# Sums of squares as float32r pairs: how the RMS statistics of a two-layer trunk are summed over partitions

## The chip, the cores and the metric

The kernel runs on one core of one Trainium2 chip. The metric is the device time of one execution in microseconds (us); of several executions the median is given. Before the change it is 2197.2 us (three runs, 2195.38 to 2199.59). PE is TensorE's matrix unit, PEld its weight loads, DVE is VectorE, ACT ScalarE, POOL GpSimd, SP the engine that issues most transfers.

## The reference

A trunk of two layers over 1024 tokens of width 1024, in float32. Layer 0 mixes tokens by latent attention (a projection to 512 + 256 + 64 columns, RMS norms of the first two parts, rotary keys, eight heads); layer 1 by an mLSTM matrix memory with four heads. Each is followed by a gated MLP with a causal convolution of width 3. Every part begins with an RMS norm and a shift and scale from the condition c, and a final norm ends the trunk:

```python
def rms_norm(x, gain=None):
    x32 = x.astype(jnp.float32)
    y = x32 * lax.rsqrt(jnp.mean(x32 * x32, axis=-1, keepdims=True) + EPS)

for i in range(DEPTH):
    h = rms_norm(x) * (1 + sc_a) + sh_a
    y = mla_mixer(h, ...) if i % N_MIXERS == 0 else mlstm_mixer(h, ...)
    x = x + g_a * y
    h = rms_norm(x) * (1 + sc_f) + sh_f
    x = x + g_f * conv_ffn(h, ...)
return rms_norm(x, final_norm)
```

The change concerns how the mean of squares in `rms_norm` is computed.

## The kernel before, in words

Activations lie transposed: 128 of the 1024 features on the partitions, tokens along the columns, eight tiles to a row block. The tokens are worked on in two halves of 512 (`hf` 0 and 1), the final norm of the second half in two groups of 256 columns. Float32 products are made of three float32r products in `mm3` (L175 to L177): each operand is split into a float32r part (`hi`) and the rest (`lo`), and hi by hi, hi by lo and lo by hi are summed in PSUM. The MLP multiplies in a form of Strassen's scheme with operands named `T1` to `T4`, `B11` and so on; its partial results carry the names `da`, `db`, `pa`, `pd`.

For a norm the sum over features runs over partitions and tiles. A `Squares` object holds a running sum `ssq` of 128 x 512: ScalarE squares a tile, VectorE adds it. The last square of a half may be kept apart (`keep`) and not added. Then `rstd_cols` forms, for each block of 128 tokens, products of `ssq` (as the weight) with a column of ones, and of the kept squares with the same column, into the PSUM tile `st` (L250): tokens now lie on partitions. VectorE makes the variance of it (`var`, L254), POOL raises it to -1/2 (`rstd`, L255), and `to_rows` transposes it, spread over 128 rows, into the tile `rb` (L262), by which VectorE multiplies the activations. These places, in order of time: `x_rows`, the norm of the input, once for each half (45 and 78 us); the norms of the query and key-value parts in `in_norms` (75 to 110 us: L494 adds a bias, L495 and L496 write the normed `cqn` and `ckvn`); both halves of the out-projection of each layer; both halves of the end of each MLP.

What sets the order: `later(n, fn, key)` queues work, here sums or transposes, and `mm3` counts the queue down by one per call, so that `fn` is emitted n sets of three products later. The counts are constants: `AFTER_SSQ`, `XW` (input norm of the second half: sums, transposes), `W0` and `WF` (MLP ends of layers 0 and 1, for each half), `X_WAIT` (out-projections), and `EVAC` (input projection: the accumulators' emptying). A tile scheduler then orders the instructions of each engine by dependences and its own priorities, so emitted order is not final order. In the part from 75 to 101 us all tiles `st` and `rb` come from a pool with one PSUM bank. The seven accumulators `ia` of the input projection are emptied by VectorE (L444, each times the row `rbs`), and the rotary query product `qrp` behind them takes a bank that one of them held. The weights for these products are split when they arrive: `whi` by ScalarE (L167) and `wlo` by VectorE (L168). At the end, L1671 multiplies the result by `rb` and the output goes out.

Of the kernel before, what the change touches and what calls it, by code (L numbers as in the profile page):

```python
# [29 lines left out]
KSCALE = 128 ** -0.5  # L30
NEG = -3.0e38
AFTER_SSQ = 6
EVAC = (7, 9)
INNER = 5
EARLY = 2

# [2 lines left out]
SCALE_ACT = ((0, 0), (1, 0), (1, 1))  # L39

STEPS = "nspppnspppoooonmooso", "nnsposppooponpmspoopo"
XW = (4, 2)
WARM = 14
W0, W0_RSTD, WF, WF_RSTD = (6, 10), (4, 3), (4, 5), (4, 4)
SHARE = 7
GATES = (2, 18, 22, 26)
MODS = (0,) * 4 + (2,) * 11 + (3,)
# [4 lines left out]
K_SHIFT = 0  # L52
AFTER_RSTD = 3
AHEAD, LOOK, RAWS, MRAWS = 4, (7, 5), 5, 2
X_WAIT, X_RSTD = (12, 3), (8, 3)
TURN = 2


# [39 lines left out]
def trunk_kernel(ctx: ExitStack, tc: tile.TileContext, xT, pos, c_d, cols_d, mod_w, win, winT, w0, w1, wf, wd, out):  # L98
# [39 lines left out]
    make_identity(nc, ident)  # L138
    ones = cst.tile([P, 1], F32, name="ones")
    pool.memset(ones, 1.0)  # L140
    nhalf = cst.tile([P, 4], F32, name="nhalf")
    pool.memset(nhalf, -0.5)
    modc = [cst.tile([P, 48], F32, name=f"modc{i}") for i in range(2)]
# [72 lines left out]
    class Squares:  # L216


        def __init__(self, p, w=HS, share=False, bufs=2, eng=None, pin=False, sqs=2):
            tile_ = lambda tag, n, size=HS: p.tile([P, size], F32, tag=f"{tag}{size}", bufs=n, name=nm(tag))[:, 0:w]  # L220
            self.w, self.n, self.share, self.eng, self.pin = w, 0, share, eng or dve, pin
            self.t = tile_("ssq", bufs, w)
            self.sq = lambda: tile_("sq", sqs, w)
            self.more = []

        def keep(self, x):

# [4 lines left out]
        def add(self, x, **kw):  # L232
# [4 lines left out]
            else:  # L237
# [2 lines left out]
                eng = pool if self.share and self.n % 2 and self.n < SHARE else self.eng  # L240
                pin(eng.tensor_tensor(self.t, self.t, sq, ALU.add))

    def rstd_cols(ssq, n, ps=None):

        st = (ps or mm_tile)("st")
        nt = ssq.w // P
        for t in range(nt):
            terms = [ssq.t, *ssq.more]
            for i, v in enumerate(terms):
                pe.matmul(st[:, t:t + 1], v[:, t * P:(t + 1) * P], ones, start=i == 0, stop=i == len(terms) - 1)  # L250
        var = cst.tile([P, 4], F32, tag="var", bufs=2, name=nm("var"))
        rstd = cst.tile([P, 4], F32, tag="rstd", bufs=2, name=nm("rstd"))
        with tc.high_priority():
            dve.tensor_scalar(var[:, 0:nt], st[:, 0:nt], 1.0 / n, EPS, ALU.mult, ALU.add)  # L254
            pool.tensor_tensor(rstd[:, 0:nt], var[:, 0:nt], nhalf[:, 0:nt], ALU.pow)  # L255
        return rstd
# [8 lines left out]
    def rstd_later(ssq, n, key, then, wait=None, ps=None, turn=AFTER_RSTD):  # L265

        def cols_():
            rstd = rstd_cols(ssq, n, ps)
            later(turn, lambda: then(to_rows(rstd, ssq.w, ps)), key)
        later(wait or AFTER_SSQ, cols_, key)  # L270

    def norm_k(p, x, rb, l, j, k, hhi, hlo):
# [228 lines left out]
    def in_norms(hf, raw, ev, ps):  # L501

        sq = [Squares(ev, bufs=4), Squares(ev, bufs=4)]
        for m in range(6):
            sq[m // 4].add(raw[:, m, :], bias=inb[:, m:m + 1])
        def rope_key():
            sl = slice(hf * HS, (hf + 1) * HS)
            t = raw[:, 6, :]
            act.activation(t, t, AF.Identity, bias=inb[:, 6:7])
            rope_apply(t, raw[:, 7, :], hf)  # L510
            act.activation(kkh[:, sl], t, AF.Copy)
            dve.tensor_tensor(kkl[:, sl], t, kkh[:, sl].bitcast(F32), ALU.subtract)
# [64 lines left out]
    class Ev:  # L577
# [292 lines left out]
    def out_proj(px, psC, osrc, us, w, l, early=0):  # L870
# [7 lines left out]
        for hf in range(2):  # L878
# [3 lines left out]
            for m in range(KT):  # L882
# [82 lines left out]
    def mlp(px, psC, T, l, u_d, pd, done, cols, extra=None, scaled=None):  # L965
# [222 lines left out]
        def d_run(i, p, w, t0=0, width=HS):  # L1188
# [14 lines left out]
            if g == len(DG) - 1 and op in ("B22", "T3", "B21", "T4"):  # L1203
                for c0, cw_ in ((0, HS),) if hf == 0 else cols:
                    if t0 <= c0 < t0 + width:
                        if (hf, c0) not in stats:
                            stats[hf, c0] = Squares(pd[0], cw_, bufs=sum(c[1] == cw_ for c in ((0, HS), *cols)),
                                                    sqs=2 if cw_ == HS else 4)
                        with tc.high_priority():
# [572 lines left out]
```

## Time and profile before

| | before |
|---|---|
| median of three runs | 2197.2 us |
| profiled execution, span | 2200.1 us (2.9 us above the median) |
| PE busy | 2166.5 us, 98% |
| DVE busy | 1693.1 us, 77% |
| ACT busy | 1046.7 us, 48% |
| POOL busy | 178.3 us, 8% |
| products into `st` for the statistics | 180 pairs of load and matmul |

The profile shows one execution of its own; its span stands for that execution's time. A row of a group gives line, engine, operation, the tile that is written and the tiles read, then a count, durations and forms. A row of a timeline gives a start, the length of the stretch to the end of the last instruction in it, and, in square brackets, the idle time of the engine ahead of it with what ended the wait. Matmul durations overlap, so the cost of one is read from start to start.

### The profile page before, as it was taken

The page shows a single profiled execution, that of the slowest core. Times are in us where ns is not written, and L with a number is a line of the kernel's source. Part 1 is how long each engine was busy: PE and PEld are TensorE (multiplying, and loading weights), DVE is VectorE, ACT ScalarE, POOL GpSimd, SP SyncE. Part 2 cuts the span into 40 slices and gives each one's busy share as a digit, 9 for nine tenths or more (in the row PEclk, how much of TensorE's full clock was granted, in tenths as well). Part 3 has the DMA queues.
Part 4 walks back from the last instruction along what each step waited for, and adds up shares of the span by engine and source line. Part 5 has one row for each costly group of instructions (what it writes and reads, how often), then busy time and mean ns, then how long its engine had stood idle before and what let it go on. Part 6 is the DMA issues. An engine that isn't in the chain of part 4 may idle for free.

```text
span 2200.1 us, 28740 instructions
## 1 busy us (share of the span) xinstructions
PE 2166.5 (98%) x10557; PEld 1818.0 (83%) x10557; DVE 1693.1 (77%) x2769; ACT 1046.7 (48%) x1812; POOL 178.3 (8%) x216
## 2 busy tenths in 40 slices
PE   9999999999999999999999999999999999999998
PEld 7878888787888888877888888988788888887787
DVE  8877878669878777899973655566887777778997
ACT  6465556446544444543453434344554444453335
POOL 0000000000000000042210111010000000002232
PEclk9999999999999999999999999999999999999999
DMA  8512234832444332542132243444143332245122
GB/s 317 152 50 63 92 109 142 285 125 69 157 139 143 123 125 85 204 151 89 53 121 93 62 131 103 132 157 171 64 144 101 111 120 92 79 163 194 50 80 77
DMA packets 105085, 270.50 MB, mean 123 GB/s; under 512 B 12336, under 2 KB 15984, under 8 KB 104944
## 3 DMA queue, kind: packets, MB, share of 16 engines
q1 hardware_dynamic: 104544, 268.28, 36.9%
q8 instruction: 83, 1.36, 0.3%
q14 instruction: 58, 0.48, 0.1%
q10 hardware_dynamic: 400, 0.39, 0.1%
HBM read 221.53 MB, written 44.47 MB: 121 GB/s over the span
## 4 chain that ended last, share of the span: by engine, by line
PE 85%; DVE 9%; DMA 3%; ACT 2%; issue 1%; POOL 0%; SPq 0%; POOLq 0%; DVEq 0%; ACTq 0%
PE pa L175 7%; PE pa L177 7%; PE pa L176 7%; PE pd L177 3%; PE pd L175 3%; PE pd L176 3%; PE sc L673 3%; PE op L175 3%; PE op L176 3%; PE op L177 2%; PE inp L177 2%; PE da L175 2%; PE inp L175 2%; PE inp L176 2%; PE da L176 2%; PE db L175 2%
## 5 line engine op out<-in xcount | busy, mean ns | idle before, releaser
L988 ACT ACTIVATE whi<-raw 128x512 fp32r<-128x512 f32 (+1 forms) x252 | 147.3, 607 | 243.2 <-PE pb L176 61.0
L988 ACT ACTIVATE whi<-wsum 128x512 fp32r<-128x512 f32 (+1 forms) x224 | 134.0, 617 | 181.8 <-PE pa L176 61.5
L175 PE MATMUL pa<-T,whi 128*128 128x512 f32 x528 | 205.9, 390 | 0.0
L176 PE MATMUL pa<-T,whi 128*128 128x512 f32 x528 | 205.4, 389 | 0.0
L177 PE MATMUL pa<-T,wlo 128*128 128x512 f32 x528 | 205.1, 389 | 0.0
L989 DVE TENSOR_TENSOR wlo<-wsum,whi 128x512 fp32r<-128x512 f32 (+1 forms) x224 | 151.1, 690 | 32.8 <-ACT whi L988 31.5
L989 POOL TENSOR_TENSOR wlo<-raw,whi 128x512 fp32r<-128x512 f32 (+1 forms) x80 | 119.9, 1515 | 401.7 <-ACT whi L988 394.0
L175 PE MATMUL da<-U,whi 128*128 128x512 f32 (+1 forms) x364 | 139.5, 383 | 3.4 <-DVE x L294 3.4
L177 PE MATMUL da<-U,wlo 128*128 128x512 f32 (+1 forms) x364 | 138.4, 383 | 2.0 <-DVE wlo L989 2.0
L176 PE MATMUL da<-U,whi 128*128 128x512 f32 (+1 forms) x364 | 139.2, 382 | 0.0
L989 DVE TENSOR_TENSOR wlo<-raw,whi 128x512 fp32r<-128x512 f32 (+1 forms) x172 | 115.7, 679 | 24.9 <-ACT whi L988 24.9
L167 ACT ACTIVATE whi<-wraw 128x1024 fp32r<-128x1024 f32 x67 | 70.7, 1059 | 117.1 <-PE op L176 59.2
L175 PEld LDWEIGHTS pa<-T,whi 128*128 128x128 f32 x528 | 99.1, 188 | 22.2 <-ACT whi L988 1.2
L177 PEld LDWEIGHTS pa<-T,wlo 128*128 128x128 f32 x528 | 99.1, 188 | 20.6
L176 PEld LDWEIGHTS pa<-T,whi 128*128 128x128 f32 x528 | 99.1, 188 | 20.3
L1140 DVE TENSOR_TENSOR U<-q,U 128x1024 fp32r<-128x1024 f32 x84 | 102.9, 1241 | 14.0 <-ACT U L1139 13.6
L1028 ACT ACTIVATE ct<-a,cols 128x512 f32<-128x512 f32 x88 | 70.8, 808 | 83.9 <-DVE a L1050 47.9
L175 PE MATMUL db<-U,whi 128*128 128x512 f32 x264 | 103.3, 391 | 1.3 <-ACT whi L988 1.3
L168 DVE TENSOR_TENSOR wlo<-wraw,whi 128x1024 fp32r<-128x1024 f32 x67 | 81.7, 1222 | 29.4 <-ACT whi L167 27.2
L177 PE MATMUL db<-U,wlo 128*128 128x512 f32 x264 | 102.9, 390 | 0.0
L176 PE MATMUL db<-U,whi 128*128 128x512 f32 x264 | 102.8, 389 | 0.0
L1139 ACT ACTIVATE U<-q 128x1024 fp32r<-128x1024 f32 x84 | 79.7, 979 | 47.7 <-DVE q L1138 22.2
(378 smaller groups left out, 6097.3 us busy)
## 6 DMA issues: line engine op xcount, KB each, us to landing
raw<-in_wf SPq DMA_DIRECT2D x96, 512.0 KB, 4.0
wraw<-in_w SPq DMA_DIRECT2D x67, 512.0 KB, 3.7
mraw<-in_mod_w SPq DMA_DIRECT2D x56, 512.0 KB, 4.0
ud<-ct SPq DMA_DIRECT2D x88, 256.0 KB, 2.4
q<-ud SPq DMA_DIRECT2D x88, 256.0 KB, 4.6
raw<-in_wd SPq DMA_DIRECT2D x32, 512.0 KB, 6.4
pa<-in_mod_w SPq DMA_DIRECT2D x24, 512.0 KB, 3.7
x<-xd SPq DMA_DIRECT2D x48, 256.0 KB, 4.8
```

The costliest lines, as they stand in the source:

```text
L167: act.activation(hi, raw, AF.Copy)
L168: dve.tensor_tensor(lo, raw, hi.bitcast(F32), ALU.subtract)
L175: pe.matmul(ps, lh, rh, start=first, stop=False, skip_group_check=more)
L176: pe.matmul(ps[:, 0:rl.shape[-1]], lh, rl, start=False, stop=False, skip_group_check=more)
L177: pe.matmul(ps, ll, rh, start=False, stop=last, skip_group_check=more)
L673: pe.matmul(ps[:, cs], a[:, qs if n < 3 else qrs_], b[:, cs], start=n == 0, stop=n == 4)
L988: act.activation(hi, src, AF.Copy)
L989: eng.tensor_tensor(lo, src, hi.bitcast(F32), ALU.subtract)
L1028: act.activation(t, a[:, 2:], AF.Identity, bias=col(f"cb{l}", m), scale=cw(m, 2))
L1139: act.activation(hi, w, AF.Copy)
L1140: dve.tensor_tensor(lo, w, hi.bitcast(F32), ALU.subtract)
```

## The change

The running sum is split into a float32r part and its rest, both in one tile `shl` (ScalarE copies, VectorE subtracts), and its sum over partitions is made by two float32r products per block with `ones2`, two columns of ones, in place of one f32 product with one column. A kept square still has its f32 product, with one column. The columns of `st` lie two apart. The last square of first halves (out-projection and MLP end of both layers) is no longer kept but added by VectorE; that of second halves stays kept, and the two last groups of 256 columns stay f32 throughout. Five constants of the order are raised, and a pool is opened earlier, so that the tile `shl` of the second half's norms can be in it.

```diff
-EVAC = (7, 9)
+EVAC = (9, 11)
-XW = (4, 2)
+XW = (6, 4)
-W0, W0_RSTD, WF, WF_RSTD = (6, 10), (4, 3), (4, 5), (4, 4)
+W0, W0_RSTD, WF, WF_RSTD = (9, 10), (4, 3), (7, 5), (4, 4)
-X_WAIT, X_RSTD = (12, 3), (8, 3)
+X_WAIT, X_RSTD = (15, 3), (8, 3)
...
+    ones2 = cst.tile([P, 2], F32R, name="ones2")
+    act.activation(ones2, ones.to_broadcast([P, 2]), AF.Copy)
...
+        def split(self):
+
+            room, tag, bufs = self.room
+            t = room.tile([P, 1024], F32R, tag=tag, bufs=bufs, name=nm("shl"))
+            hi, lo = [t[:, i * HS:i * HS + self.w] for i in range(2)]
+            act.activation(hi, self.t, AF.Copy)
+            dve.tensor_tensor(lo, self.t, hi.bitcast(F32), ALU.subtract)
+            self.pair = hi, lo
...
+        terms = [(v, ones2) for v in ssq.pair] if ssq.pair else [(ssq.t, ones)]
+        terms += [(v, ones) for v in ssq.more]
         for t in range(nt):
-            terms = [ssq.t, *ssq.more]
-            for i, v in enumerate(terms):
-                pe.matmul(st[:, t:t + 1], v[:, t * P:(t + 1) * P], ones, start=i == 0, stop=i == len(terms) - 1)
+            for i, (v, one_) in enumerate(terms):
+                pe.matmul(st[:, 2 * t:2 * t + one_.shape[-1]], v[:, t * P:(t + 1) * P], one_, start=i == 0,
+                          stop=i == len(terms) - 1, skip_group_check=len(terms) > 2)
...
+        if not ssq.more:
+            ssq.split()
         later(wait or AFTER_SSQ, cols_, key)
...
+        if hf == 1:
+            sq[0].room = sq[1].room = pa, "shl", 1
...
+    stA, pa = phase("pa", side="right")
     in_norms(1, rawB, Ev(), None)
-    stA, pa = phase("pa", side="right")
...
-                ssq.keep(x[:, m, :]) if m == KT - 1 else ssq.add(x[:, m, :])
+                if hf and m == KT - 1:
+                    ssq.split()
+                    ssq.keep(x[:, m, :])
+                else:
+                    ssq.add(x[:, m, :])
...
-                            if op in ("T3", "T4") and (p == 3 or p == 2 and c0 > 0):
+                            if op == "T4" and (p == 3 or p == 2 and c0 > 0):
+                                if cw_ == HS:
+                                    stats[hf, c0].split()
                                 stats[hf, c0].keep(xs[hf][:, m, c0:c0 + cw_])
```

The rows below are the order of one engine's instructions in the built program. A row has the line, the operation, the tile written and the tiles read (with a number for each tile) and the size; lines of the changed kernel are some 2 to 23 higher.

TensorE in the input projection of the second half, at the sums of squares of the query part (`st_690`, then `st_716`) and the key-value part (`st_707`, `st_735`) and of the second half's input norm (`st_716`, then `st_748`), to the first transposes. Before:

```order
L250 MATMUL st_690<-ones,ssq_641 128x1 x4
L177 MATMUL ia_502<-h_458,winl_107 128x512
L175 MATMUL ia_503<-h_458,winh_106 128x512
L176 MATMUL ia_503<-h_459,winh_106 128x512
L250 MATMUL st_707<-ones,ssq_642 128x1 x4
L177 MATMUL ia_503<-h_458,winl_107 128x512
L175 MATMUL ia_504<-h_458,winh_106 128x512
L250 MATMUL st_716<-ones,ssq_115 128x1 x4
L176 MATMUL ia_504<-h_459,winh_106 128x512
L177 MATMUL ia_504<-h_458,winl_107 128x512
L262 MATMUL rb_728<-ident,rstd_696 128x128 x4
```

and after, with the rows between left out from the second sums on:

```order
L262 MATMUL st_716<-ones_77,shl_678 128x2
L178 MATMUL ia_513<-h_461,winh_108 128x512
L179 MATMUL ia_513<-h_460,winl_109 128x512
L177 MATMUL ia_514<-h_460,winh_108 128x512
L262 MATMUL st_716<-ones_77,shl_678 128x2 x7
...
L262 MATMUL st_735<-ones_77,shl_681 128x2 x7
...
L262 MATMUL st_748<-ones_77,shl_707 128x2 x7
L177 MATMUL ia_512<-h_460,winh_110 128x512
L178 MATMUL ia_512<-h_461,winh_110 128x512
L276 MATMUL rb_764<-ident,rstd_726 128x128 x4
```

Each sum is now eight products instead of four, the first of them ahead of the other seven, with wide products between; counted over the projection, the first `rb` stands 17 wide products later. The second half's input norm has its `rb` between the last wide products before, and behind all of them, directly ahead of the first `qrp`, after.

VectorE from the first use of `rb` to the emptying of the accumulators. Before:

```order
L494 SCALAR_TENSOR_TENSOR raw_470<-raw_470,inb,rb_751 128x512
L168 TENSOR_TENSOR wlo_784<-wraw_781,whi_783 128x1024
L168 TENSOR_TENSOR wlo_790<-wraw_787,whi_789 128x1024
L496 SCALAR_TENSOR_TENSOR ckvn_668<-raw_470,cols,ckvn_668 128x512
L494 SCALAR_TENSOR_TENSOR raw_470<-raw_470,inb,rb_751 128x512
L496 SCALAR_TENSOR_TENSOR ckvn_668<-raw_470,cols,ckvn_668 128x512
L444 TENSOR_TENSOR raw_843<-ia_500,rbs_767 128x512
```

and after:

```order
L170 TENSOR_TENSOR wlo_826<-wraw_823,whi_825 128x1024
L512 SCALAR_TENSOR_TENSOR ckvn_677<-raw_479,cols,ckvn_677 128x512
L494 TENSOR_TENSOR raw_479<-raw_479,cs_638 128x512
L495 TENSOR_TENSOR raw_479<-raw_479,cs_639 128x512
L510 SCALAR_TENSOR_TENSOR raw_479<-raw_479,inb,rb_787 128x512
L496 TENSOR_TENSOR raw_479<-raw_479 128x512
L170 TENSOR_TENSOR wlo_1589<-wraw_1586,whi_1588 128x1024
L512 SCALAR_TENSOR_TENSOR ckvn_677<-raw_479,cols,ckvn_677 128x512
L460 TENSOR_TENSOR raw_873<-ia_509,rbs_803 128x512
```

L444 became L460. Ahead of the first of them now stand four weight rests (`wlo`, two of them above the rows shown) instead of two, and the three rotary steps of the key (L494 to L496 of the changed kernel, which stood behind the emptying as L478 to L480).

VectorE at the end of the program, where `rb_18782` and `rb_18863` belong to the first group of 256 columns, `rb_18821` and `rb_18902` to the second. Before:

```order
L1671 TENSOR_TENSOR x_17142<-x_17142,rb_18637 128x1024
L294 SCALAR_TENSOR_TENSOR x_17070<-da_18289,modc_80,x_17070 128x256
L1671 TENSOR_TENSOR x_17070<-x_17070,rb_18782 128x2x256 x2
L254 TENSOR_SCALAR var_18817<-st_18810 128x2
L1671 TENSOR_TENSOR x_17070<-x_17070,rb_18782 128x2x256 x2
L1671 TENSOR_TENSOR x_17070<-x_17070,rb_18821 128x2x256 x4
```

and after:

```order
L268 TENSOR_SCALAR var_18842<-st_18837 128x2
L243 TENSOR_TENSOR ssq_18670<-ssq_18670,sq_18850 128x256
L1694 TENSOR_TENSOR x_17219<-x_17219,rb_18737 128x1024
L268 TENSOR_SCALAR var_18898<-st_18891 128x2
L1694 TENSOR_TENSOR x_17147<-x_17147,rb_18863 128x2x256 x4
L1694 TENSOR_TENSOR x_17147<-x_17147,rb_18902 128x2x256 x4
```

The first group's four products, of which two stood ahead of the second group's variance, now all stand behind it.

More of the change, by code (lines that the diff above doesn't have):

```diff
@@ L223, in __init__ @@
             self.sq = lambda: tile_("sq", sqs, w)
-            self.more = []
+            self.more, self.pair, self.room = [], None, (p, "shl", 1)
         def keep(self, x):
@@ L246, in rstd_cols @@
         nt = ssq.w // P
+        terms = [(v, ones2) for v in ssq.pair] if ssq.pair else [(ssq.t, ones)]
+        terms += [(v, ones) for v in ssq.more]
         for t in range(nt):
-            terms = [ssq.t, *ssq.more]
-            for i, v in enumerate(terms):
-                pe.matmul(st[:, t:t + 1], v[:, t * P:(t + 1) * P], ones, start=i == 0, stop=i == len(terms) - 1)
+            for i, (v, one_) in enumerate(terms):
+                pe.matmul(st[:, 2 * t:2 * t + one_.shape[-1]], v[:, t * P:(t + 1) * P], one_, start=i == 0,
+                          stop=i == len(terms) - 1, skip_group_check=len(terms) > 2)
+        st = st[:, 0:2 * nt].rearrange("p (t o) -> p t o", o=2)[:, :, 0:1].rearrange("p t o -> p (t o)")
         var = cst.tile([P, 4], F32, tag="var", bufs=2, name=nm("var"))
@@ L1208, in d_run @@
                                                     sqs=2 if cw_ == HS else 4)
+                            stats[hf, c0].room = px, "raw", RAWS
                         with tc.high_priority():
-                            if op in ("T3", "T4") and (p == 3 or p == 2 and c0 > 0):
+                            if op == "T4" and (p == 3 or p == 2 and c0 > 0):
+                                if cw_ == HS:
+                                    stats[hf, c0].split()
                                 stats[hf, c0].keep(xs[hf][:, m, c0:c0 + cw_])
```

## Prediction

> **What bounds the kernel now.** I read the page's head, its busy shares and its chain first, then what TensorE waits for, then the groups of the tile `st`, and last the timeline at each place where the change moves something.
>
> ```profile
> span 2200.1 us, 28740 instructions
> PE 2166.5 (98%) x10557; PEld 1818.0 (83%) x10557; DVE 1693.1 (77%) x2769; ACT 1046.7 (48%) x1812; POOL 178.3 (8%) x216
> ...
> PE 85%; DVE 9%; DMA 3%; ACT 2%; issue 1%; POOL 0%; SPq 0%; POOLq 0%; DVEq 0%; ACTq 0%
> ```
>
> TensorE is busy for 98% of the span and holds 85% of the chain that ended last. So a TensorE instruction removed in a full stretch is worth its own time, and a TensorE wait added anywhere is paid in full, unless a later wait swallows it. Of its waits (sum in us, times, longest), these lie at work that the change touches:
>
> ```profile
> PE kp L175 <- ACT ckvn L495: 1.9, 1, 1.9
> ...
> PE rb L262 <- POOL rstd L255: 1.7, 3, 1.1
> ...
> PE qrp L175 <- ACT cqn L495: 0.6, 1, 0.6
> ...
> PE inp L176 <- DVE h L278: 0.4, 1, 0.4
> ```
>
> The transposes `rb` wait 1.7 us in all for POOL's powers, and the norm work behind them (`kp`, `qrp`) another 2.5 for ScalarE. Waits are small already; there is more to lose than to win.
>
> **What the products cost.** The program has 90 such f32 products; the profile has each as two pairs of a weight load and a matmul, 180 pairs:
>
> ```profile
> L250 PE MATMUL st<-ones,ssq x96: 164/250/250, 44.7 to 2190.7; 128*128 128x1 f32 x96
> L250 PEld LDWEIGHTS st<-ones,sq x68: 186/192/333, 448.3 to 2191.2; 128*128 128x128 f32 x68
> ...
> L250 PE MATMUL st<-ones,ev x16: 164/250/250, 103.3 to 104.9; 128*128 128x1 f32 x16
> ```
>
> ```profile
> 2171.28 0.28 PE L250 MATMUL st<-ones,ssq 128*128 128x1 f32 x2
> ...
> 2173.06 0.47 PE L175 MATMUL db<-U,whi 128*128 128x512 f32 x1
> ```
>
> Eight products (a sum and one kept square, four column groups) take 1.78 us, 0.22 each. Of float32r products with two columns the trace has none. The nearest rows are the weight loads of two wide ones:
>
> ```profile
> 449.82 0.19 PEld L175 LDWEIGHTS op<-oh,whi 128*128 128x128 f32 x1
> 449.93 0.19 PEld L176 LDWEIGHTS op<-ol,whi 128*128 128x128 f32 x1
> ```
>
> These float32r loads follow each other after 0.11 us, and last 0.19 us as the f32 loads of `st` do. I take 0.11 us: half an f32 product. Below that lies the transpose, 0.09 (four from 79.40 to 79.75, quoted further on); above, 0.22, if two columns were no cheaper. After the change there are 104 float32r products and 22 f32 ones (the 256-wide groups of the end, and the kept square of second halves).
>
> By the Trainium skill, "TensorE: Matmul & The Clock Gate", section "Weight-path perf modes — Fast Weight Load (FWL) and DoubleRow", weights of 128 columns that are not FP32 load in a fast mode. If float32r counted as not FP32, at half of 0.11 us the sum would be 5.7 us lower; the equal 188 and 192 ns of the rows speak against it here.
>
> **Where pairs really go.** A sum alone cost four f32 products and now costs eight float32r ones: 0.89 against 0.89, nothing won. That holds for the four norms and for both `x_rows`. Second halves with a kept square have 8 float32r and 4 f32 against 8 f32: nothing again. Only where VectorE now adds the last square do 16 pairs become 8: first halves of both out-projections and of both MLP ends. That is 0.89 us at each of four places, 3.6 us in all. At three (448, 1509, 2171 us) the products stand nine matmuls or more later than before and their transposes still later, so the added square and the split have 2 us of matmuls to hide behind: **-2.7 us**. In the layer-0 MLP end `rb` comes 1.15 us later by the order (nine matmuls of 0.23, less the shorter block), and the input products behind it already wait 0.4 us for h. I put 0.9 us of new waits there: **0**, bounds -0.9 and +0.8.
>
> **What it adds off TensorE.**
>
> ```profile
> L988 ACT ACTIVATE whi<-raw 128x512 fp32r<-128x512 f32 (+1 forms) x252 | 147.3, 607 | 243.2 <-PE pb L176 61.0
> ...
> L989 DVE TENSOR_TENSOR wlo<-wsum,whi 128x512 fp32r<-128x512 f32 (+1 forms) x224 | 151.1, 690 | 32.8 <-ACT whi L988 31.5
> ```
>
> Thirteen splits of 607 ns on ScalarE and 690 on VectorE, and four more adds: 7.9 and 11.7 us, on engines at 48% and 77%. Where TensorE has its next matmuls ready, this costs nothing; uncovered, one split costs 1.3 us. `ones2` and its table load sit in the start's wait for a transfer: 0.
>
> **First x_rows (45 us).**
>
> ```profile
> 44.70 0.95 PE L250 MATMUL st<-ones,ssq 128*128 128x1 f32 x8
> ...
> 47.91 0.65 PE L262 MATMUL rb<-ident,rstd 128*128 128x128 f32 x4
> ```
>
> ```profile
> 46.00 1.85 POOL L255 TENSOR_TENSOR rstd<-var,nhalf 128x4 f32<-128x4 f32 x1 [44.60 <-DVE var L254]
> ```
>
> Nine matmuls (2.1 us) stand between sums and transposes now, and just cover var and the 1.85 us power: 47.91 is a 0.2 us gap. The order after has five (1.15 us). The last sum to `rb` takes about 2.5 us with the same power, so TensorE waits 0.9 us more: **+0.9**, carried into the next place.
>
> **Norms and second x_rows (75 to 125 us).** All `st` and `rb` here share one PSUM bank.
>
> ```profile
> 79.40 0.60 PE L262 MATMUL rb<-ident,rstd 128*128 128x128 f32 x4
> 79.75 0.48 PE L175 MATMUL ia<-h,winh 128*128 128x512 f32 x1
> ...
> 96.49 0.39 PE L175 MATMUL qrp<-cqn,whi 128*128 128x512 f32 x1
> ```
>
> ```profile
> 80.03 2.06 DVE L494 SCALAR_TENSOR_TENSOR raw<-raw,inb,rb 128x512 f32<-128x512 f32 x3 [0.78 <-PE rb L262]
> ...
> 86.86 2.36 DVE L168 TENSOR_TENSOR wlo<-wraw,whi 128x1024 fp32r<-128x1024 f32 x2
> ...
> 92.66 1.32 DVE L444 TENSOR_TENSOR raw<-ia,rbs 128x512 f32<-128x512 f32 x2 [0.57 <-PE ia L177]
> ...
> 98.01 0.68 DVE L478 TENSOR_TENSOR raw<-raw,cs 128x512 f32<-128x512 f32 x1
> 98.61 0.69 DVE L479 TENSOR_TENSOR raw<-raw,cs 128x512 f32<-128x512 f32 x1
> ```
>
> Before, the first `rb` starts at 79.40, and 0.63 us later VectorE starts six bias adds, six norm products and two weight rests, 12.6 us with its waits, then empties the accumulators (92.66) before `qrp` needs one of their banks. After, the order gives `rb` 17 matmuls more ahead of it: 17 x 0.23 + 0.9 puts it at 84.2, and I add 0.8 for waits on the three splits, 85.0. VectorE's list ahead of the emptying grows by two weight rests (2 x 1.13, next start to start) and three rope steps (3 x 0.6): 85.6 + 12.6 + 4.1 = 102, less about 1.3 of its present waits, filled by them: near 101. `qrp` stands behind the third `rb` and needs an emptied bank: 101.7 instead of 96.49, **+5.2** there, with TensorE idle for about 4 us.
>
> What follows was already bound by VectorE, whose third column after PE and PEld reads 5.00 from 110 to 115:
>
> ```profile
> 100.00:105.00 5.00, 5.00 (x33) 4.42 (x31) 3.67 (x7) 3.19 (x6) 0.41 (x1) 1.00 0.16 37
> 105.00:110.00 5.00, 4.71 (x40) 4.51 (x40) 4.56 (x8) 2.52 (x5) 1.57 (x2) 1.00 0.51 101
> 110.00:115.00 5.00, 3.52 (x14) 2.02 (x12) 5.00 (x9) 2.64 (x5) 0.00 (x0) 1.00 0.19 75
> 115.00:120.00 5.00, 3.35 (x10) 2.85 (x11) 3.93 (x10) 4.04 (x6) 0.00 (x0) 0.57 0.44 128
> 120.00:125.00 5.00, 5.00 (x20) 4.17 (x19) 3.34 (x12) 2.13 (x8) 0.00 (x0) 0.75 0.13 29
> ```
>
> ```profile
> 116.65 0.79 PE L175 MATMUL kp<-ckvn,whi 128*128 128x512 f32 x1 [1.93 <-ACT ckvn L495]
> 117.24 1.05 PE L673 MATMUL sc<-kk,qr 128*128 128x256 f32 x4
> ...
> 118.62 0.63 PE L176 MATMUL qp<-cqn,whi 128*128 128x512 f32 x1
> 119.05 0.63 PE L177 MATMUL qp<-cqn,wlo 128*128 128x512 f32 x1
> ...
> 124.29 0.39 PE L177 MATMUL kp<-ckvn,wlo 128*128 128x512 f32 x1
> ```
>
> The emptying starts 8.3 us later. VectorE's 1.8 us of idle between 100 and 110 give a part back, one weight rest has left its list and two splits' rests have joined it (-1.1, +1.2): the first scores come near 123.5, **+6**. But the granted clock there is 0.57 and 0.75 after the gaps: matmuls start 0.43 us apart instead of 0.23 for some 7.6 us, which costs 3.6 us now. If the new waits are spread so that the clock stays, the same point is reached at only +2.4. Bounds +2.4 and +6 with the first x_rows in it; I take **+5**, nearer the upper, because a second stretch of gaps remains.
>
> **The end.**
>
> ```profile
> 2191.69 0.16 DVE L254 TENSOR_SCALAR var<-st 128x2 f32<-128x2 f32 x1 [0.70 <-PE st L250]
> 2191.77 1.28 DVE L1671 TENSOR_TENSOR x<-x,rb 128x512 f32<-128x512 f32 x2
> ...
> 2193.41 2.48 DVE L1671 TENSOR_TENSOR x<-x,rb 128x512 f32<-128x512 f32 x4 [0.36 <-PE rb L262]
> ```
>
> Of the first group's four final products the last two run behind this last var, and the second group's four end at 2195.9. By the order after, all matmuls precede the first group's sums (no count of the two last groups is edited; the scheduler moved them), and VectorE has all eight products after the last var: about 2191.9 + 0.2 + 8 x 0.62 = 2197.0, **+1.1**. Nothing hides it.
>
> **Sum.** -2.7 + 0 + 5 + 1.1 = +3.4 us: 2203.5 on the profiled execution's 2200.1. That one lies 2.9 us above the median of 2197.2, so I predict 2200.6. A difference under 0.2% (4.4 us) can't be told from none in this kernel.
>
> **Rivals.**
> *The clock closes once more* (slower). The idle at 97.5 to 101.7 is as long as the stretch of gaps that ends at 116.65, behind which the clock fell. If it falls at 101.7 too, and TensorE rather than VectorE then decides, 3.6 us come on top of +6: 6 + 3.6 - 2.7 + 1.1 = +8, 2205. Without the second fall but at the full +6, +4.4 is the edge. It decides from 4 us of idle on. Against it: VectorE's lateness partly hides a slow TensorE there. The skill's page on TensorE, section "The HAM clock gate", says that an idle window of about 3.4 us halves the clock, which speaks for this rival; the trace halves it after shorter gaps with matmuls between (116.65).
> *The waits don't come* (faster). If ScalarE and VectorE take the norm work in time, the removed pairs stand: -3.6, less 0 to 1 at the end; with products as cheap as a transpose, 104 x 0.02 = 2 us more. 2191 to 2194.
> *The products don't shrink*: two pairs each for float32r too, 72 pairs more instead of 32 fewer, 104 x 0.11 = +11.4 us on the sum, 2212. Against it: the loads at 449.82 and 449.93 belong to two products, one load each; 3%.
>
> **Chances.** No measurable change (the sum, +2.4 to +4.4, and its milder mixtures) 0.42; slower by over 0.2% (the clock, the full +6, or the doubled pairs) 0.34; faster by over 0.2% (waits hidden) 0.24. Eight in ten: 2191.5, where the hidden waits and 0.11 us end, to 2207, above the second fall. The likeliest case alone: 2198 to 2202.
>
> **What would show it.** Right: `st` has 148 pairs, the float32r ones 0.11 us apart; the four blocks that now hold eight are 0.9 us shorter; `qrp` begins near 101.7 behind an accumulator emptied near 101, and the first scores near 123; VectorE's last eight products form one block. Wrong: `qrp` still at 97 to 98, or a granted clock of 1.00 from 115 to 125, which makes the kernel faster; two-column products 0.05 or 0.2 us apart; long waits at 448, 1509 or 2171.

## The result: 20 us slower, and most of it where nothing was edited

The changed kernel takes 2215.7 us (median of five runs, 2214.69 to 2216.58) against 2196.1 us of the kernel before beside it: a ratio of 1.0083, 95% interval 1.0071 to 1.0096. The prediction was 2200.6 us with a range of 2191.5 to 2207.0. It is wrong in size and in kind: no measurable change was forecast, and the change costs 0.8%.

The page of the profile after, its head, busy shares and chain:

```profile
span 2214.0 us, 28704 instructions
PE 2174.9 (98%) x10525; PEld 1816.5 (82%) x10525; DVE 1701.6 (77%) x2786; ACT 1056.7 (48%) x1827; POOL 175.1 (8%) x216
...
PE 82%; DVE 10%; DMA 3%; ACT 3%; issue 2%; SPq 0%; POOL 0%; DVEq 0%; ACTq 0%; POOLq 0%
```

TensorE has 32 matmuls fewer, as it should (10557 before), and yet is busy for 8.4 us longer. That is the line to stop at: waits would show as idle time, but here the work itself became slower. The windows view says where. One window in the middle of the first MLP, before and after:

```profile
650.00:700.00 50.00, 50.00 (x222) 41.42 (x221) 40.31 (x67) 22.24 (x38) 0.30 (x3) 1.00 0.47 154
```

```profile
650.00:700.00 50.00, 50.00 (x220) 40.92 (x219) 39.01 (x65) 21.48 (x36) 0.30 (x3) 1.00 0.37 124
```

TensorE is busy throughout, at a granted clock of 1.00, both times; it starts 222 matmuls in 50 us before and 220 after. No statistic is summed anywhere near. The timeline of TensorE there, before (a group of products with the operand B):

```profile
650.63 0.39 PE L175 MATMUL pd<-B,whi 128*128 128x512 f32 x1
650.86 0.39 PE L176 MATMUL pd<-B,whi 128*128 128x512 f32 x1
...
652.45 0.39 PE L177 MATMUL pd<-B,wlo 128*128 128x512 f32 x1
```

and after, behind a group with the operand T:

```profile
656.78 0.39 PE L177 MATMUL pa<-T,whi 128*128 128x512 f32 x1
...
659.27 0.39 PE L179 MATMUL pa<-T,wlo 128*128 128x512 f32 x1
659.50 0.40 PE L177 MATMUL pd<-B,whi 128*128 128x512 f32 x1
659.73 0.40 PE L178 MATMUL pd<-B,whi 128*128 128x512 f32 x1
...
662.06 0.40 PE L179 MATMUL pd<-B,wlo 128*128 128x512 f32 x1
```

Twelve products with B take 2.80 us from start to start (659.50 to 662.30, the start of the next group) where twelve with T take 2.72 (656.78 to 659.50), and both took 2.72 before. So 233 ns against 227 for the same form of product. One of the groups `pa<-T` in each round of seven shows 233 too, so two of seven groups are slow, through both MLPs.

What differs is where things lie. In the built program the 8 bytes of `ones2` take a slot of 32 bytes, and the weight tiles `whi` and `wlo` and most operands lie 32 bytes further than before; the operands B22 and T3 lie at the other end of the memory and did not move. Their products are the slow ones.

The other losses are where the prediction looked for them. TensorE's waits after, those at the changed work:

```profile
PE rb L276 <- POOL rstd L269: 7.0, 7, 1.9
...
PE qrp L177 <- DVE raw L460: 2.3, 1, 2.3
...
PE rb L276 <- DVE raw L510: 0.8, 1, 0.8
...
PE st L262 <- DVE shl L251: 0.5, 1, 0.5
```

The transposes wait 7.0 us for POOL's powers instead of 1.7. A span, from the first to the last instruction, is 1.7 us shorter than the time of its execution (2214.0 against 2215.7 here). By that the profiled execution of the changed kernel was at its median and that of the kernel before some 5.7 us above its own (an estimate), so the spans differ by only 13.9 us; the sums below go by the timed runs.

### The profile page after: what moved, and what is told of

Read it like the earlier page. It is cut to its first block, busy times and chain, and to the rows that moved or that the text cites. A ratio compares the mean times of both kernels' runs of the same rounds, so it can differ in the third digit from the quotient of the medians.

```text
span 2214.0 us, 28704 instructions
## 1 busy us (share of the span) xinstructions
PE 2174.9 (98%) x10525; PEld 1816.5 (82%) x10525; DVE 1701.6 (77%) x2786; ACT 1056.7 (48%) x1827; POOL 175.1 (8%) x216
## 4 chain that ended last, share of the span: by engine, by line
PE 82%; DVE 10%; DMA 3%; ACT 3%; issue 2%; SPq 0%; POOL 0%; DVEq 0%; ACTq 0%; POOLq 0%
PE pa L177 7%; PE pa L178 7%; PE pa L179 7%; PE pd L179 3%; PE pd L177 3%; PE pd L178 3%; PE sc L689 3%; PE op L177 2%; PE op L178 2%; PE op L179 2%; PE inp L179 2%; PE inp L178 2%; PE inp L177 2%; PE da L177 2%; PE da L178 2%
## 5 line engine op out<-in xcount | busy, mean ns | idle before, releaser
L178 PE MATMUL inp<-h,whi 128*128 128x512 f32 x256 | 101.3, 396 | 0.5 <-DVE h L294 0.5
```

Source lines behind the costliest of these rows:

```text
L178: pe.matmul(ps[:, 0:rl.shape[-1]], lh, rl, start=False, stop=False, skip_group_check=more)
```

## The experiments

All times are medians; the kernel before ran beside them at 2195.3 to 2196.2 us. Three questions: is it the place in memory, what rule of place, and what does each part of the change cost without it.

### The place alone: 32 and 64 bytes in the kernel before, 96 more in the changed one

```diff
     pool.memset(ones, 1.0)
+    pad = cst.tile([P, 8], F32, name="pad")
```

Nothing reads or writes `pad`; in the second run it has 16 columns.

> The kernel before with 32 unused bytes allocated per partition where the change allocates its two columns of ones; no instruction is added, and the order of every engine is the same. Theory placement: the change's 32 bytes move the weights and most operands of the MLP products, while the operands B22 and T3 on the other side of the memory stay, and products of a moved weight with an unmoved operand then start 0.2335 us apart instead of 0.2267 (1044 products in pd and pa, and their neighbours). It expects 8.4 us more than the kernel before (about 2204.5), with the slow rows at the same products as in the changed kernel. Rival, the splits or the other changed work slow these products: no change, 2196 +- 2.

Measured: 2206.9 us, ratio 1.0050 (1.0038 to 1.0063), 11.6 us more than the kernel before (8.3 to 13.8 by the interval). No instruction and no order was changed. The products with B are at 233 ns here too:

```profile
652.82 0.40 PE L176 MATMUL pd<-B,whi 128*128 128x512 f32 x1
653.05 0.40 PE L177 MATMUL pd<-B,whi 128*128 128x512 f32 x1
...
655.39 0.40 PE L178 MATMUL pd<-B,wlo 128*128 128x512 f32 x1
```

The theory had said 8.4 us. The rival, that the changed work slows them, falls.

> As the run before, with 64 unused bytes. If the products are slow whenever weight and operand lie at different places modulo 128 bytes, 8 us more than before again. If only 32 bytes modulo 64 count, no change: 2196 +- 2. The rival that the changed work slows the products expects no change too.

Measured: 2204.2 us, ratio 1.0040 (1.0027 to 1.0052). So not 32 bytes modulo 64: 64 bytes are slow as well, which fits a modulus of 128 or more.

> The changed kernel with 96 unused bytes behind the two columns of ones, so that all tiles behind it lie 128 bytes further than in the kernel before; the order of every engine is the changed kernel's. Theory placement: the products with B22 and T3 are at 0.2267 us again, 8.4 us off the changed kernel's 2215.7, about 2207, and what is left over the kernel before (some 11 us) is the norms at 75 to 125 us (8), and the end (1 to 2). Rival, the changed work slows them: 2215 +- 2.

Here `pad` has 24 columns and stands behind `ones2` in the changed kernel. Measured: 2212.1 us, ratio 1.0077 (1.0063 to 1.0091). It is neither what the theory said (2207) nor quite the rival's 2215. The trace decides: the products with B22 and T3 were still slow, at 232.6 ns. A modulus of 128 falls.

To find the rule I took the float32r products of 128x512 with a weight `whi`, `wlo`, `winh` or `winl` whose successor followed without a wait, in each trace, and looked up in the built program how far the weight and the operand lie apart, modulo 256 bytes. The table gives the count and the mean start to start; products that could not be matched to the program one by one are left out, which makes some counts smaller.

| kernel | distance 0 | other distances |
|---|---|---|
| before | 7433 at 227.1 ns | none |
| changed | 6035 at 227.4 | 32: 301 at 233.1; 224: 1044 at 233.5 |
| before + 32 | 6028 at 227.5 | 32: 302 at 233.2; 224: 1044 at 233.4 |
| before + 64 | 6110 at 227.4 | 64: 297 at 229.2; 192: 1044 at 233.3 |
| changed + 96 | 6106 at 227.3 | 128: 1346 at 232.6 |

In the kernel before each of these weights lies a multiple of 256 bytes from its operand. Each kernel with a displacement has two kinds of slow products: the 1044 of B22 and T3, and some 300 more, which with 32 and 64 bytes are all in the input projection (`ia`). With 32 bytes that is, by the rows, 1044 x 6.3 + 302 x 6.1 ns = 8.4 us, and 2.4 us more for the others (6028 at 227.5 instead of 227.1; many of these stand behind a slow group): 10.8 of the 11.6 us.

The score and value products of the attention (`sc`, `pv`) are not in the table, and the rule does not show there. Those of 128x512 start 230 to 233 ns apart at any distance: `pv` at 232.1 ns with distance 0 in the kernel before and at 232.1 with 224 in the changed one; in the kernel before `sc` at 230.6 with distance 0 (101 products) and at 230.8 with 128 (50 products, those with `kk` and `qr`). What makes these slower than 227 ns was not looked into.

### The rule: 256 bytes, and distance and not place

The changed kernel with 56 columns of `pad`, so that everything moves by 256 bytes:

> The changed kernel with 224 unused bytes, 256 with the columns of ones; the order is the changed kernel's. With 32, 64 and 128 bytes the products whose weight and operand lie at different places modulo 256 bytes were the slow ones, and only those. Theory, the modulus is 256: no slow product is left, 8 to 9 us off the changed kernel's 2215.7 and 5 off the run with 128 bytes: 2205 to 2207. Rival, the modulus is 512 or there is no such rule and any displacement of the two sides against each other is slow: 2212 to 2215.

Measured: 2203.8 us, ratio 1.0034 (1.0022 to 1.0047): 11.9 us off the changed kernel's time with 224 unused bytes (11.5 when each is taken against the kernel before that ran beside it), 1.2 us below what the theory said. Every product of the table's kind is at distance 0, at 227.2 ns. The rival falls.

The kernel before with the 32 bytes, and 224 at the other end of the memory:

```diff
+    far = ctx.enter_context(tc.tile_pool(name="far", bufs=1, side="right"))
+    far_pad = far.tile([P, 56], F32, name="far_pad")
     crow = cst.tile([P, D], F32, name="crow")
```

> The kernel before with the 32 unused bytes that cost 11.6 us, and 224 more at the other end of the memory, where B22 and T3 lie, so that these move 224 bytes down while the weights move 32 up: 256 bytes against each other. Same order on every engine. Theory: what counts is the distance of weight and operand modulo 256 bytes, not where either lies: no slow product, 2195 to 2197 as before. Rival, the weights' own place counts: 2204 to 2207 as with the 32 bytes alone.

Measured: 2195.0 us, ratio 0.9992 (0.9983 to 1.0001), the kernel before's time, with the weights where they cost 11.6 us in the first run of this series. The same group in its trace:

```profile
650.04 0.39 PE L178 MATMUL pd<-B,whi 128*128 128x512 f32 x1
650.27 0.39 PE L179 MATMUL pd<-B,whi 128*128 128x512 f32 x1
...
652.53 0.39 PE L180 MATMUL pd<-B,wlo 128*128 128x512 f32 x1
```

So what counts for these products is the distance of weight and operand modulo 256 bytes. Why the memory or TensorE is slower at other distances, no run here shows.

### The parts of the change, with the place restored

Without the split sums in the four norms and both input norms (their f32 products and their two constants as before):

```diff
-        if not ssq.more:
+        if not ssq.more and n == D and key is not ssq:
             ssq.split()
```

> The changed kernel with the 96 bytes, but without the split sums in the four norms and in both input norms (those stay one f32 product per block), and with the two order constants of that part as before; the order of VectorE up to the first out-projection is again the kernel's before. What is left of the change are the out-projections and the MLP ends. Theory: all of the loss at 75 to 125 us comes from the splits in the norms, so scores start at 117.2 us as before; the four shorter blocks give 2.7 to 3.6 us and the end takes up to 2: 2194 to 2196. Rival, the splits at the out-projections and MLP ends cost more than the pairs give: 2198 or above.

This ran with 128 bytes, before the rule was known: 2203.5 us, ratio 1.0042 (1.0030 to 1.0055), above what its theory said, with the slow products still in it. With 256 bytes:

> Split sums at the out-projections and MLP ends alone (norms and input norms f32, two constants as before), with the 256 bytes. Theory: the 2203.5 of the same kernel with 128 bytes loses its slow products (7 to 8 us): 2195 to 2196.5, the same as before, because the two out-projections give 0.9 each, the first MLP end nothing, and the last MLP end's 0.9 is lost with 2 to 3 us at the end. If the splits cost nothing anywhere, 2192.

Measured: 2196.6 us, ratio 1.0000 (0.9991 to 1.0009), at the upper end of what the theory said. The splits of the norms and input norms, together with the two constants raised for them (`EVAC` and `XW`), therefore cost 7.2 us (2203.8 - 2196.6).

Then both MLP ends as in the kernel before, so that only the out-projections are changed:

```diff
-                            if op == "T4" and (p == 3 or p == 2 and c0 > 0):
-                                if cw_ == HS:
-                                    stats[hf, c0].split()
+                            if op in ("T3", "T4") and (p == 3 or p == 2 and c0 > 0):
```

> As the run before, with both MLP ends as in the kernel before (last square kept, f32, old constants there), so only the two out-projections are split and shortened. Theory: 0.9 us at each, no loss at the end: 2193 to 2194, 0.1% under the kernel before. If the end's loss does not come from the split of the last MLP end, it stays: 2195 to 2197.

Measured: 2193.0 us, ratio 0.9987 (0.9978 to 0.9995). This version beats both kernels: the 0.9 us at each out-projection are there (2.7 us, 1.1 to 4.8 by the interval), and both MLP ends together cost 3.6 us.

Which of the two ends costs what (here `l` is the layer; the constant of the first end, `W0`, is as before too):

```diff
-                            if op == "T4" and (p == 3 or p == 2 and c0 > 0):
-                                if cw_ == HS:
+                            if op in ((("T3", "T4"), ("T4",))[l]) and (p == 3 or p == 2 and c0 > 0):
+                                if cw_ == HS and l == 1:
                                     stats[hf, c0].split()
```

> The run with split out-projections (2193.0), and of the two MLP ends only the last one as changed (added, split, its constant raised), with the 256 bytes. Theory: its first half saves 0.9 us of products, but the final products of the second half queue up on VectorE behind the last variance, which costs 2.2: 1.3 us more than 2193.0, about 2194.3; the other 1.3 to 2.3 of the 3.6 us between the runs with and without both ends belong to the first MLP end. Rival, all 3.6 us come at the end: 2196.6.

Measured: 2195.4 us, ratio 0.9998 (0.9990 to 1.0007), between the theory (2194.3) and the rival (2196.6). Of the 3.6 us, 2.4 come at the end and 1.2 at the first MLP end. Differences of one or two microseconds between two medians whose runs spread over 3 to 5 us carry little more than their sign, so the traces stand beside them. From the start of the 400th product of the MLP, counted from its last, to the end of the program they read 97.7 us with the out-projections alone, 99.0 with both MLP ends split and 99.6 with the last one alone: 1.3 to 1.9 us lost at the end. VectorE at the end, in the kernel with the out-projections alone:

```profile
2182.47 1.27 DVE L1693 TENSOR_TENSOR x<-x,rb 128x512 f32<-128x512 f32 x2
2184.10 2.48 DVE L1693 TENSOR_TENSOR x<-x,rb 128x512 f32<-128x512 f32 x4 [0.36 <-PE rb L277]
```

and with both MLP ends split:

```profile
2185.32 0.16 DVE L269 TENSOR_SCALAR var<-st 128x2 f32<-128x2 f32 x1 [1.32 <-PE st L263]
2185.39 4.86 DVE L1695 TENSOR_TENSOR x<-x,rb 128x512 f32<-128x512 f32 x8
```

Eight final products in one block, behind the last variance, where six stand behind it otherwise. At the first MLP end the transposes wait for the power: TensorE's waits from 1080 to 1160 us with both ends split, and in the kernel with the out-projections alone:

```profile
PE rb L277 <- POOL rstd L270: 1.4, 2, 1.0
PE inp L179 <- DVE h L295: 0.5, 1, 0.5
```

```profile
PE rb L277 <- POOL rstd L270: 0.3, 1, 0.3
```

1.6 us of waits more, against a block 0.9 us shorter. In two other traces with this MLP end unsplit, that of the kernel before and that with the last end alone, the waits there sum to 0.9 us, so the split adds 1.0 to 1.6.

### Which of the early splits costs the 7.2 us

The norms split, the input norms not; and the other way round:

```diff
-        if not ssq.more:
+        if not ssq.more and key is not ssq:      # the first run; in the second: and n == D
             ssq.split()
```

> The changed kernel with the 256 bytes, with the input norms of both halves f32 again and everything else (four norms split, both constants raised) as changed. In its order VectorE empties the accumulators behind three weight rests, without the rotary steps, and the third transposes stand twenty matmuls ahead of the rotary product. Theory: the loss at 75 to 125 us needs the three splits together, which crowd one bank and VectorE; with two of them the rotary product starts by 98, and the first scores by 121: 4 to 5 us less than the changed kernel with 256 bytes, 2201 +- 2. Rival, each split costs its own share there: two thirds of the 8 us stay, 2203 to 2204.

Measured: 2199.7 us, ratio 1.0021 (1.0012 to 1.0031): 3.1 us above the run with neither. That favoured the theory that it takes all three splits.

> The changed kernel with the 256 bytes, with the four norms f32 again and both input norms split. In its order VectorE empties the accumulators behind three weight rests and without the rotary steps. Theory: the first input norm costs 1 us (its transposes wait for the power), the second nothing, so 1 us more than the run without any of these splits (2196.6): 2197 to 2198; with the norms' 3.1 us that leaves 3 of the 7.2 us to the three together. Rival, the second input norm alone brings the late emptying: 2200 or above.

Measured: 2200.4 us, ratio 1.0016 (1.0007 to 1.0025): 3.8 us above. My theory said 1 and falls, and with it the reading of the run before. The rival's time came, 2200 or above, but not its mechanism: no wait for the accumulators' emptying stands before `qrp` in this trace (98.26 us).

3.1 + 3.8 = 6.9, nearly all of 7.2. But this is no sum of splits alone. Both runs keep `EVAC` and `XW` raised, and the run with neither split has them as before, so whatever the two constants cost is counted in both. In `rstd_later` these constants are the counts ahead of the sums: `XW` for the input norms of both halves, `EVAC` for the query and the key-value norm (the description ahead of the prediction has both otherwise). At the first input norm, with it split (VectorE's row of the split, then TensorE's) and in the run where it is f32:

```profile
39.64 0.68 DVE L252 TENSOR_TENSOR shl<-ssq,shl 128x512 fp32r<-128x512 f32 x1
...
45.06 0.95 PE L263 MATMUL st<-ones,shl 128*128 128x2 f32 x8
...
48.48 1.01 PE L277 MATMUL rb<-ident,rstd 128*128 128x128 f32 x4 [1.19 <-POOL rstd L270]
```

```profile
48.98 0.65 PE L277 MATMUL rb<-ident,rstd 128*128 128x128 f32 x4 [1.59 <-POOL rstd L270]
```

The wait is there without a split too, and the split is done 5 us before the sums. What changed here is the order: the sums stand six wide products later, and five or six wide products instead of nine are left behind them to cover the power. In the built program `XW` raised alone moves them so, and `EVAC` raised alone does not. From the 101st to the 251st product of the input projection the traces read 36.7 us with `XW` as before, 38.3 with it raised and this norm f32, and 38.0 with it raised and this norm split (the changed kernel with 256 bytes). So 1.5 us at this place come without a split, and the split adds nothing that shows. In the run with both input norms split it is 39.5, because the clock fell there as well: granted 0.50 from 49 to 52 us, products 0.43 us apart.

At the norms of the second half the split itself is in the chain. The longest such wait there with the norms split, and in the kernel without these splits:

```profile
112.16 0.65 PE L277 MATMUL rb<-ident,rstd 128*128 128x128 f32 x4 [1.92 <-POOL rstd L270]
```

```profile
104.65 0.65 PE L277 MATMUL rb<-ident,rstd 128*128 128x128 f32 x4 [0.29 <-POOL rstd L270]
```

There a split puts two more instructions, on two engines, between the last add and the sum, and TensorE stands at the transposes behind it. And one thing stands only where all three are split: TensorE waits 1.58 us before the third transposes and 2.29 us for the emptying before `qrp` (the changed kernel with 256 bytes); with the norms or the input norms alone neither wait is there. From the 101st product of the input projection to the first of the out-projection the traces read 349.1 us with neither, 352.8 with the norms split, 354.4 with the input norms and 359.5 with all: 3.7 + 5.3 against 10.4, with the 1.5 us of `XW` counted in both parts. That speaks for an interplay of the three. But these are single executions, and the medians show 7.2 us for the 10.4. No run has the raised constants without any of these splits, so how the 7.2 us divide stays open.

In the changed kernel, as in the run with the norms split, the second half's two norms also share one tile `shl`: ScalarE's second split waits 1.85 us for TensorE to read the first (the changed kernel's timeline of ScalarE, and then of TensorE):

```profile
113.25 0.63 ACT L250 ACTIVATE shl<-ev 128x512 fp32r<-128x512 f32 x1 [1.85 <-PE st L262]
```

```profile
117.92 1.11 PE L276 MATMUL rb<-ident,rstd 128*128 128x128 f32 x4 [1.85 <-POOL rstd L269]
```

```diff
-            sq[0].room = sq[1].room = pa, "shl", 1
+            sq[0].room = sq[1].room = pa, "shl", 2
```

> The changed kernel with the 256 bytes and two tiles shl instead of one for the norms of the second half; all else as changed. In the changed kernel ScalarE's second split there waits 1.85 us until TensorE has read the first one's tile (113.25 us), and the two norms run one behind the other. Theory: that shared tile is part of the 7.2 us at 40 to 135 us; with two tiles the second power, transposes and norm come up to 1.9 us earlier and the first scores with them: 2202 to 2202.5 against 2203.8. Rival: VectorE, late with the accumulators, sets the pace there, and nothing moves: 2203.8 +- 0.8.

Measured: 2204.5 us, ratio 1.0032 (1.0020 to 1.0044), the same as with one tile. In its trace the transposes come 2.8 us earlier than with one tile; both rows, two tiles first:

```profile
115.71 0.65 PE L277 MATMUL rb<-ident,rstd 128*128 128x128 f32 x4 [0.77 <-POOL rstd L270]
```

```profile
118.55 1.11 PE L277 MATMUL rb<-ident,rstd 128*128 128x128 f32 x4 [1.85 <-POOL rstd L270]
```

The first scores come 2.3 us earlier; the time does not show it. Of the 2.8 us, 1.4 are there already at 110 us, ahead of the shared tile (110.13 instead of 111.56 at the first products of `sc`), where the clock stayed low for 7 products of `qrp` instead of 13 of `qrp` and `kp`. The other 1.4 fit the tile. The runs spread from 2200.4 to 2205.6, so a gain of 1 to 2 us can't be excluded. The run is inconclusive. The three splits ahead of `qrp` share one tile as well; more tiles there were not tried.

## Why the prediction was wrong, point by point

| term | forecast | measured |
|---|---|---|
| place of weights and operands | not in the sum | +11.9 |
| norms and input norms with their two constants, 40 to 135 us | +5 | +7.2 |
| two out-projections | -1.8 | -2.7 |
| first MLP end | 0 | +1.2 |
| last MLP end and the end | -0.9 + 1.1 | +2.4 |
| sum | +3.4 | +20.0 (19.6 between the medians) |

**The step that failed** is the sentence "`ones2` and its table load sit in the start's wait for a transfer: 0". It priced the instructions of `ones2` and not its 32 bytes. What the runs showed in its place is 11.9 us from 32 bytes of displacement. All working behind it took the 227 ns of every untouched product for granted. The views shown with the prediction could not have told the price: in the kernel before all 7433 products of the table lie at distance 0, so it has no row slowed by a displacement. The displacement itself could have been read from the built program.

**Products.** Two float32r products with two columns were put at 0.11 us each. TensorE at the first out-projection, changed kernel:

```profile
458.72 0.95 PE L262 MATMUL st<-ones,shl 128*128 128x2 f32 x8
459.53 0.47 PE L177 MATMUL op<-oh,whi 128*128 128x512 f32 x1
```

Eight take 0.81 us, 0.10 each, where sixteen f32 pairs took 1.78, and `st` has 148 pairs, as forecast. The rival of the doubled pairs falls, and the rule of the Trainium skill ("TensorE: Matmul & The Clock Gate", section "Weight-path perf modes — Fast Weight Load (FWL) and DoubleRow") does not show for float32r here: the loads of `shl` last 191 ns on the mean, like the 191 of `ssq` in f32.

**The input projection** went as worked out, within 0.4 us, up to `qrp`:

```profile
84.64 0.60 PE L276 MATMUL rb<-ident,rstd 128*128 128x128 f32 x4
...
98.63 0.62 PE L276 MATMUL rb<-ident,rstd 128*128 128x128 f32 x4 [0.84 <-DVE raw L510]
101.54 0.50 PE L177 MATMUL qrp<-cqn,whi 128*128 128x512 f32 x1 [2.29 <-DVE raw L460]
...
127.02 0.75 PE L689 MATMUL sc<-kk,qr 128*128 128x256 f32 x4 [0.65 <-DVE qr L641]
```

```profile
100.80 2.48 DVE L460 TENSOR_TENSOR raw<-ia,rbs 128x512 f32<-128x512 f32 x4
```

`rb` at 84.6 (85.0 forecast), emptying at 100.8 (101), `qrp` at 101.5 (101.7). Counted from one product early in the projection, the 101st, so that the starts of the executions cancel, these three come 5.7, 8.6 and 5.5 us later than in the kernel before (5.6, 8.3 and 5.2 forecast), and with the place restored 5.2, 8.6 and 5.5. So this is no luck of the slow products: VectorE's list and the wait of `qrp` behind it came as read from the order. At the first input norm TensorE waits 1.05 us behind five wide products, near the 0.9 worked out. Then the forecast for the first scores (123.5) missed by 3.5 us. I had taken VectorE for the bound between the emptying and the scores, from windows of the kernel before. After, the third column after PE and PEld reads otherwise:

```profile
100.00:105.00 5.00, 3.46 (x11) 2.83 (x12) 5.00 (x10) 3.72 (x7) 0.00 (x0) 0.80 0.33 105
105.00:110.00 5.00, 5.00 (x20) 3.90 (x19) 3.77 (x7) 2.06 (x4) 0.00 (x0) 0.86 0.31 77
110.00:115.00 5.00, 3.89 (x31) 3.56 (x30) 2.53 (x5) 1.75 (x3) 1.01 (x1) 1.00 0.13 31
115.00:120.00 5.00, 3.15 (x21) 3.06 (x20) 3.02 (x6) 2.73 (x5) 1.45 (x1) 0.67 0.00 0
120.00:125.00 5.00, 5.00 (x20) 4.28 (x20) 4.69 (x8) 2.98 (x6) 0.00 (x0) 0.65 0.00 0
```

VectorE is idle for 4.4 of the 10 us from 110 to 120, and TensorE for 3.0: the two norms run as one chain, split, sum, variance, power, transposes, each waiting for the one before. A longer chain was priced as work on a busy engine (1.2 us of added VectorE work), where its latency counts.

**The rival "the clock closes once more"** came true as a mechanism: the granted clock falls twice, to 0.80 and 0.86 behind the idle before 101.5, and to 0.67 and 0.65 again. That its 2205 is close to the 2203.8 with the place restored is luck in part: it put 9.6 us at the norms, where 7.2 came, and -1.6 at the out-projections and ends, where +0.9 came. The first fall is where the Trainium skill ("TensorE: Matmul & The Clock Gate", section "The HAM clock gate") puts one, behind an idle window of about 3.4 us: between the end of the input projection (97.8 us) and `qrp` (101.5) TensorE did only four transposes. The fall at 49 us in the run with the input norms split came behind a wait of 1.19 us, so a stretch as long as that is not needed for every fall. In the changed kernel's trace eight products behind the first fall are 0.43 us apart instead of 0.23, which is 1.6 us; how many of the 7.2 us are the clock's was not separated.

**The ends.** At the out-projections the cover was there, as argued. At the first MLP end the new waits were put at 0.9 us, and 1.0 to 1.6 came; the +1.2 lies above the upper bound of 0.8, by less than the runs spread. At the last one the eight products in one block stand exactly as read from the order; but the cost around them is 2.4 instead of 0.2, one part of it a wait of 0.5 us for `shl` that I had ruled out (the row of TensorE's waits above).

## What to carry to other kernels

Before pricing what a change computes, check what it moves: compare the places of weights and operands in the built program before and after, because a tile of 8 bytes cost 12 us here, and 224 unused bytes gave them back. When a busy engine shows longer busy time for fewer instructions, compare start to start of the same form in a stretch that nobody edited, before looking at the stretch that was. And price a step put into a chain that others wait for as latency, not as load: at the norms of the second half the transposes wait 1.9 us behind splits that sit on engines at 48% and 77%, while at the out-projections, behind 2 us of ready matmuls, the runs show no cost. A count in the order that is raised to give such a step room has its own price: at the first input norm it cost 1.5 us, and the split, done 5 us before the sums, needed no room.

## What the hardware showed that I had not expected

In the projections and MLPs a float32r product of 128x512 starts 227.1 ns after the one before it when weight and operand lie a multiple of 256 bytes apart, and 232.6 to 233.5 ns when they lie 32, 128, 192 or 224 bytes off that; only one group of 297, at 64 bytes, was in between (229.2). The attention's score and value products start 230 to 233 ns apart at distance 0 as well as off it. The clock has no part in the MLP's difference (1.00 in the windows from 650 to 700 us). The groups behind a slow one are a little slower too (228 to 229 ns on the mean of twelve).

POOL's power over 128x4 numbers took 1.01 us in most places of the kernel before and 1.85 and 1.93 in two (46.0 and 1112.8 us), and it stands in every one of these chains.
